# Root steps and sums of squares through PSUM, GpSimd's order pinned in one stage, the opening reordered, and a norm's two sums moved to VectorE

## The chip, the cores and the metric

One core of one Trainium2 chip. The metric is the time of one execution on the device, in microseconds (us), the median of three runs. Engines by the profile's names: PE is TensorE (its weight loads are PEld), DVE is VectorE, ACT is ScalarE, POOL is GpSimd, SP issues the DMAs. Matrix products accumulate in PSUM banks of 128 x 512 fp32; all else lives in SBUF.

## The reference

Two transformer blocks in fp32, on 512 positions of width 1024. The first has a sparse attention and a gated convolution that are merged, then a convolutional feed-forward net; the second has two mixer layers (grouped-query plus latent attention, then windowed attention). The change touches only norms, and the order of work around them:

```python
def rms_norm(x, g):
    xf = x.astype(jnp.float32)
    y = xf * lax.rsqrt(jnp.mean(xf * xf, axis=-1, keepdims=True) + NORM_EPS)
    return (y * g.astype(jnp.float32)).astype(x.dtype)
...
        h = rms_norm(x, norm1_g[l])
        proj = h @ w_in[l]
        ...
        g_a, g_b = jnp.split(jax.nn.sigmoid(g_merge), 2, axis=-1)
        x = x + (g_a * y_attn + g_b * y_conv) @ w_out[l]
        x = x + conv_ffn(rms_norm(x, norm2_g[l]), ffn_w_up[l], ffn_dw_w[l], ffn_dw_b[l], ffn_w_down[l])
    return rms_norm(x, final_g)
```

The first norm of the second block is taken of the first block's output, which is itself normed by `final_g`; so the kernel needs two sums per position there, of x*x and of x*x times the squared gain.

## The kernel before

The residual stream lies as eight tiles `X[k]` of 128 features by 512 positions. A matrix product is done by `mm3` (L121): each fp32 operand is split into a high and a low part, and three matmuls (L124 to L126) per 128 rows of weights sum up low times high, high times low and high times high. Weights come by `wload` (L97): a DMA brings a raw tile, ScalarE makes the high part (L110), and GpSimd or VectorE, by a rotating table `wpools`, subtracts it to get the low part (L111). A tile-scheduling framework orders the instructions of each engine by their readiness; inside `in_order(...)` the named engines keep the order in which the code is written, and `after_root()` holds what follows until the instruction in `root[0]`.

A norm goes in four steps. `Squares.add` (L220): ScalarE squares a tile (L222), and `put` lets VectorE add it to a running sum in SBUF (L212 for the first pair, L215 for the others); the last tile is kept apart. `sums` (L225): TensorE multiplies both parts with ones (L232), so that the sums over features stand one position per partition, 128 x 4 or 128 x 2 numbers. `rsqrt` and `newton` (L160 to L183): VectorE scales and adds eps (L183), takes a first guess by integer arithmetic (L164) and improves it in two rounds (L167 to L173), eight dependent small instructions, all in SBUF. `row_bcast` (L189): TensorE turns the roots into a row on all partitions, which `to_sbuf` copies (L195).

In the opening, TensorE multiplies four 128-column groups of weights: two in banks `pkv`, then `pkb[0]` and `pkb[1]`. The sums stand in the middle of `pkb[0]`'s matmuls, the broadcast behind them. The row R1 then scales `tkv` (L354) and `tkb` (L437), the latter of which frees the banks for the w_v product. `windows` (L153, L381) lays out the keys for the compression.

In the gates stage (`gates`, called with `in_order("PE", "DVE")`) 14 products `w_g` of 24 matmuls run, with two weight tiles each; between them VectorE and GpSimd add the taps of a 31-tap convolution. For the first channel tile ScalarE scales the shifted input (L487) and GpSimd adds it (L488); the order on GpSimd is the scheduler's.

In the first norm of the second block, `by_halves` runs the last product of the feed-forward net (w_dn) for the first 256 positions, eight blocks of rows of 12 matmuls with 256 columns, and then for the other 256. `down` adds each block to X (L842), squares it, and `Weighted` (L234) lets TensorE multiply the squares with a two-column weight (ones and squared gain) into bank `po` (L248). After a half come L850 to L852, the root, the broadcast, and `modulated` (L817 to L819) for eight tiles. While the root of a half is awaited TensorE goes on with the next half or with `key_values`. `attn_out` and `last_out`, further on, work by halves in the same way with `Squares`.

Of the kernel before, what the change touches and what calls it, by code (L numbers as in the profile page):

```python
# [43 lines left out]
def build(ctx, tc, I, out):  # L44
# [136 lines left out]
    def rsqrt(src, scale, eps):  # L181
        x = new("s", (128, 20))[:, :src.shape[1]]
        V.tensor_scalar(x, src, scale, eps, op0=OP.mult, op1=OP.add)  # L183
        return newton(x)
# [12 lines left out]

    class Squares:


        def __init__(self, a=0, b=512):
            self.c = slice(a, b)
            self.acc = self.last = None
# [16 lines left out]
        def add(self, src, scale=1.0):  # L220
            t = new("p")
            A.activation(t[:, self.c], src[:, self.c], AF.Square, scale=scale)  # L222
            self.put(t)

        def sums(self, bank="ps"):  # L225
            st = new(bank)
            n = (self.c.stop - self.c.start) // 128
            for x in (self.acc, self.last):
                for i in range(n):

                    a = self.c.start + 128 * i
                    PE.matmul(st[:, i:i + 1], x[:, a:a + 128], ones[:, 0:1], start=x is self.acc and i == 0,  # L232
                              stop=x is self.last, skip_group_check=True)
            return st[:, 0:n]  # L234

    class Weighted:


        def __init__(self, a, w):
            self.c, self.w, self.n, self.st = slice(a, a + 256), w, 0, new("po")  # L240

        def add(self, src):
            t = new("p")
            A.activation(t[:, self.c], src[:, self.c], AF.Square)
            k = self.n
            for i in range(2):

                PE.matmul(self.st[:, 2 * i:2 * i + 2], t[:, self.c][:, i * 128:(i + 1) * 128], self.w[:, k, :],  # L248
                          start=k == 0 and i == 0, stop=k == KT - 1, skip_group_check=True)
            self.n += 1  # L250
# [1122 lines left out]
```

## Time and profile before

| what | us |
|---|---|
| median of three runs | 1309.24 |
| lowest and highest of them | 1303.06, 1313.09 |
| the profiled execution | 1305.09 |
| its span, first to last instruction | 1303.1 |
| TensorE busy | 1248.2 |
| VectorE busy | 893.2 |
| GpSimd busy | 729.7 |
| ScalarE busy | 701.7 |

The mean granted clock of TensorE was 0.992 of full speed. The busy times are of the profiled execution. A row of a timeline gives the start and the length of an instruction in us, or of several alike in a row (x4), and in brackets how long its engine had been idle before it and whose instruction ended the wait. Since matmuls are pipelined, their rows overlap; the distance of their starts is what one costs.

### The profile page before, as it was taken

What the parts mean: (1) busy time and instruction counts of PE and PEld (TensorE: products, weight loads), DVE (VectorE), ACT (ScalarE), POOL (GpSimd) and SP (SyncE); (2) the same over time, 40 slices, a digit from 0 to 9 for tenths busy, and PEclk for the clock granted to TensorE, in tenths of its full rate; (3) what the DMA queues carried; (4) which work ended last, traced back from release to release, by engine and by line L of the source; (5) the groups of instructions that cost most, each with busy time, mean ns of one, the idle gap of its engine ahead of it and who ended that gap; (6) DMA issues with size and microseconds to landing.
All of it is one profiled execution on the core that took longest, in us unless ns stands there. A gap on an engine that the chain in (4) does not pass through costs nothing. (4 is left out here: it accounts for less than half of the span.)

```text
span 1303.1 us, 19296 instructions
## 1 busy us (share of the span) xinstructions
PE 1248.2 (96%) x6369; PEld 1039.2 (80%) x6369; DVE 893.2 (69%) x1967; ACT 701.7 (54%) x1487; POOL 729.7 (56%) x715
## 2 busy tenths in 40 slices
PE   7899999799999999999999999999999989999996
PEld 5878877688888888888888798877777788888886
DVE  7755767697645777776877358677787776655565
ACT  6756777334543444423443243586677646776654
POOL 4457785844644666565665513477565423676542
PEclk9999999899999999999999999999999999999998
DMA  6231011332443555587553501211111111111221
GB/s 209 78 97 58 33 59 33 122 98 87 124 123 97 161 170 161 163 252 240 165 162 87 160 16 40 72 39 50 47 60 42 41 50 57 57 57 57 67 72 65
DMA packets 71971, 124.74 MB, mean 96 GB/s; under 512 B 8256, under 2 KB 17344, under 8 KB 71872
## 3 DMA queue, kind: packets, MB, share of 16 engines
q1 hardware_dynamic: 71872, 123.52, 30.5%
q8 instruction: 50, 0.82, 0.3%
q14 instruction: 49, 0.40, 0.1%
HBM read 121.39 MB, written 2.10 MB: 95 GB/s over the span
## 5 line engine op out<-in xcount | busy, mean ns | idle before, releaser
L111 POOL TENSOR_TENSOR wl<-wr,wh 128x512 fp32r<-128x512 f32 (+2 forms) x215 | 281.9, 1314 | 266.7 <-ACT wh L110 208.9
L124 PE MATMUL pg<-h,wl 128*128 128x512 f32 x628 | 249.3, 397 | 2.8 <-POOL wl L111 2.7
L126 PE MATMUL pg<-h,wh 128*128 128x512 f32 x628 | 246.7, 393 | 0.0
L125 PE MATMUL pg<-h,wh 128*128 128x512 f32 x628 | 246.5, 393 | 0.0
L110 ACT ACTIVATE wh<-wr 128x512 fp32r<-128x512 f32 (+2 forms) x215 | 132.5, 618 | 174.9 <-PE pg L126 83.0
L124 PEld LDWEIGHTS pg<-h,wl 128*128 128x128 f32 x628 | 118.4, 188 | 26.6 <-POOL wl L111 4.1
L126 PEld LDWEIGHTS pg<-h,wh 128*128 128x128 f32 x628 | 118.4, 189 | 23.0
L125 PEld LDWEIGHTS pg<-h,wh 128*128 128x128 f32 x628 | 118.5, 189 | 22.2 <-issue 0.7
L111 POOL TENSOR_TENSOR m<-t,m 128x512 fp32r<-128x512 f32 (+1 forms) x67 | 89.5, 1336 | 80.4 <-ACT m L110 78.3
L304 DVE TENSOR_TENSOR t<-pt,t 128x512 fp32r<-128x512 f32 (+1 forms) x160 | 97.4, 631 | 27.0 <-ACT t L303 25.8
L309 PE MATMUL po<-t,h 128*128 128x512 f32 (+3 forms) x384 | 110.0, 364 | 4.3 <-DVE t L304 1.9
L124 PE MATMUL ps<-h,wl 128*128 128x512 f32 x260 | 103.4, 398 | 7.4 <-POOL wl L111 7.4
L126 PE MATMUL ps<-h,wh 128*128 128x512 f32 x260 | 102.0, 392 | 0.0
L125 PE MATMUL ps<-h,wh 128*128 128x512 f32 x260 | 102.0, 392 | 0.0
L303 ACT ACTIVATE t<-pt 128x512 fp32r<-128x512 f32 (+1 forms) x160 | 84.4, 552 | 22.8 <-PE pt L299 22.1
L309 PEld LDWEIGHTS po<-t,h 128*128 128x128 f32 x384 | 65.7, 188 | 28.8 <-ACT t L303 13.2
L299 PE MATMUL pt<-k,p 128*128 128x128 f32 x576 | 85.5, 273 | 2.7 <-POOL p L976 2.5
L299 PEld LDWEIGHTS pt<-k,p 128*128 128x128 f32 x576 | 69.0, 140 | 14.3 <-POOL p L976 5.0
L744 DVE CUSTOM_DVE_ANT_0 b<-b,z 128x512 f32<-128x512 f32 x48 | 75.4, 1572 | 0.0
L976 POOL TENSOR_SCALAR p<-p,s 128x512 f32<-128x512 f32 x64 | 45.5, 713 | 49.8 <-DVE s L975 49.7
L124 PEld LDWEIGHTS ps<-h,wl 128*128 128x128 f32 x260 | 49.2, 189 | 20.2 <-POOL wl L111 10.1
L110 ACT ACTIVATE m<-t 128x512 fp32r<-128x512 f32 (+2 forms) x78 | 46.9, 604 | 33.7 <-PE ps L124 12.9
(404 smaller groups left out, 3050.9 us busy)
## 6 DMA issues: line engine op xcount, KB each, us to landing
b<-ada_t SPq DMA_DIRECT2D x48, 256.0 KB, 3.2
z<-ada_t SPq DMA_DIRECT2D x48, 256.0 KB, 3.2
t<-w_up SPq DMA_DIRECT2D x44, 256.0 KB, 2.8
wr<-w_up SPq DMA_DIRECT2D x44, 256.0 KB, 2.7
wr<-w_g SPq DMA_DIRECT2D x32, 256.0 KB, 2.6
t<-w_dn SPq DMA_DIRECT2D x23, 256.0 KB, 2.7
wr<-w_br SPq DMA_DIRECT2D x16, 256.0 KB, 2.7
wr<-w_gt SPq DMA_DIRECT2D x16, 256.0 KB, 2.8
```

Of the source, the lines that this page charges most:

```text
L110: A.activation(hi[:, :z], raw[:, :z], AF.Copy)
L111: eng.tensor_sub(lo[:, :z], raw[:, :z], f(hi[:, :z]))
L124: PE.matmul(ps, ll, rh, start=start and i == 0, stop=False)
L125: PE.matmul(ps, lh, rl, start=False, stop=False)
L126: PE.matmul(ps, lh, rh, start=False, stop=stop and i == n - 1)
L299: PE.transpose(ps[:, o:o + 128], src, ident)
L303: evac[:] = [A.activation(hi[:, :n], ps[:, :n], AF.Copy)]
L304: evac.append(V.tensor_sub(lo[:, :n], ps[:, :n], f(hi[:, :n])))
L309: PE.matmul(o[:, a:b], v, t[:, pa:pa + b - a], start=start and z == 0, stop=stop and z == 1)
L744: V.tensor_tensor_reduce(out=raw, in0=raw, in1=CA[z], op0=OP.mult, op1=OP.add, scale=1.0, scalar=0.0, accum_out=MA[l][:, z, m:m + 1])
L976: scaled[0] = G.tensor_scalar(p, p, sm[:, 1:2], 0.0, op0=OP.mult, op1=OP.add)
```

## The change

Its parts, with the line numbers of the new kernel where they differ:

- `newton` (now L160 to L179) has eleven instructions: the guess is written twice (L168), to PSUM and to SBUF, the value after the first round too (L174), and one step is split in two (L177, L178). Its temporaries lie in columns of a PSUM bank, that of the sums or a new `po`.
- `Squares.add` writes the first square into a PSUM bank (`pt`), and VectorE adds the following ones there (L245); the add of the last but one goes to SBUF, and the last square goes to TensorE by itself as before. `sums` is L256 and its banks are `pt` or `po`.
- Opening: the sums come after two instead of four rows of `pkb[0]`, the w_v weights don't wait for the root, all eight of their low parts are GpSimd's, `tkb[0]` (L443) stands ahead of the windows.
- `gates(0, 7, ...)` is written under `in_order("Pool")` as well. Taps are L497 now.
- `down`: `Weighted` is gone; VectorE keeps a plain sum (L245) and a weighted sum (L856, L861) in two `pt` banks, and TensorE sums each once per half.

```diff
-    def newton(x):
+    def newton(x, bank=None):
         n = x.shape[1]
-        y = new("s", (128, 20))[:, :n]
-        t = new("s", (128, 20))[:, :n]
-        V.tensor_scalar(y.bitcast(I32), x.bitcast(I32), -0.5, float(0x5F3759DF), op0=OP.mult, op1=OP.add)
-        V.tensor_mul(t, y, y)
+        r, q, u = [new("s", (128, 20))[:, :n] for _ in range(3)]
+        st = bank or work[0]
+        y = st[:, 64:64 + n]
+        t = st[:, 128:128 + n]
+        for z in (y, r):
+            V.tensor_scalar(z.bitcast(I32), x.bitcast(I32), -0.5, float(0x5F3759DF), op0=OP.mult, op1=OP.add)
+        V.tensor_mul(t, y, r)
         V.scalar_tensor_tensor(t, t, -0.5 * 0.375, x, op0=OP.mult, op1=OP.mult)
-        V.scalar_tensor_tensor(y, t, 1.5 * 0.375, y, op0=OP.add, op1=OP.mult)
-        V.tensor_mul(t, y, y)
+        for z in (y, q):
+            V.scalar_tensor_tensor(z, t, 1.5 * 0.375, r, op0=OP.add, op1=OP.mult)
+        V.tensor_mul(t, y, q)
         V.scalar_tensor_tensor(t, t, 64.0 / 9, x, op0=OP.mult, op1=OP.mult)
-        V.scalar_tensor_tensor(t, t, -10.0 / 3, t, op0=OP.add, op1=OP.mult)
-        root[:] = [V.scalar_tensor_tensor(y, t, 5.0, y, op0=OP.add, op1=OP.mult)]
-        return y
+        V.tensor_scalar(u, t, -10.0 / 3, None, op0=OP.add)
+        V.tensor_mul(t, t, u)
+        root[:] = [V.scalar_tensor_tensor(r, t, 5.0, q, op0=OP.add, op1=OP.mult)]
+        return r
...
-        def add(self, src, scale=1.0):
+        def add(self, src, scale=1.0, bank="pt"):
+            i, c = self.n, self.c
+            self.n += 1
+            if i == 0:
+                self.sum = new(bank)
+                A.activation(self.sum[:, c], src[:, c], AF.Square, scale=scale)
+                return
             t = new("p")
-            A.activation(t[:, self.c], src[:, self.c], AF.Square, scale=scale)
-            self.put(t)
+            A.activation(t[:, c], src[:, c], AF.Square, scale=scale)
+            if i == self.of - 1:
+                self.last = t
+            else:
+                acc = self.sum
+                if i == self.of - 2:
+                    self.acc = new("z", (128, 542))[:, 0:512]
+                    acc = self.acc
+                V.tensor_add(acc[:, c], self.sum[:, c], t[:, c])
+            return t
...
-        mm3(pkb[0], wk[0][:4], xg[:4], True, False)
+        mm3(pkb[0], wk[0][:2], xg[:2], True, False)
         r1 = rsqrt(total.sums("pt"), 1.0 / D, EPS)
-        mm3(pkb[0], wk[0][4:], xg[4:], False, True)
+        mm3(pkb[0], wk[0][2:], xg[2:], False, True)
...
-    with after_root():
-        wv = wsplit(I["w_v"], KT, 280, ("m", "h"))
+    wpools[0] = [("t", "wh", "wl", G), ("wr", "wh", "wl", G)]
+    wv = wsplit(I["w_v"], KT, 280, ("m", "h"))
+    wpools[0] = [("t", "wh", "wl", G), ("t", "wh", "wl", V), ("wr", "wh", "wl", G)]
...
+    tkb = [new("p") for _ in range(2)]
+    root[:] = [V.tensor_mul(tkb[0], pkb[0], R1)]
     with after_root():
         ZK = windows(tkv[0], cv("pek", 0, 16))
-    tkb = []
-    for b in range(2):
-        tkb.append(new("p"))
-        V.tensor_mul(tkb[b], pkb[b], R1)
+    V.tensor_mul(tkb[1], pkb[1], R1)
...
     with in_order("PE", "DVE"):
-        gates(0, 7, 0, 90)
+        with in_order("Pool"):
+            gates(0, 7, 0, 90)
...
     def down(th, m, ps, c):
         if m == 0:
-            sums.append(Weighted(256 * th, fg2))
+            sums.append((Squares(256 * th, 256 * th + 256), new("pt")))
         V.tensor_add(X[m][:, c], X[m][:, c], ps)
-        sums[th].add(X[m])
+        total, weighted = sums[th]
+        t = total.add(X[m])
+        w = weighted[:, c]
+        if m == 0:
+            V.tensor_scalar(w, total.sum[:, c], fg2[:, m, 1:2], None, op0=OP.mult)
+            return
+        if m == KT - 1:
+            weighted = new("z", (128, 542))[:, 0:512]
+            sums[th] = (total, weighted)
+        V.scalar_tensor_tensor(weighted[:, c], t[:, c], fg2[:, m, 1:2], w, op0=OP.mult, op1=OP.add)
```

How the instructions stand now, at three places. First VectorE in the opening, before: from the copy of the row R1 (L195), which stands 15 instructions after the root's last, to the product that frees the first bank (L437).

```order
L195 COPY r_333<-pt_328 128x512
L372 TENSOR_TENSOR h_475<-k_107,h_474 128x8
L354 TENSOR_TENSOR p_360<-pg_208,r_333 128x512
L354 TENSOR_TENSOR p_362<-pg_209,r_333 128x512
L153 TENSOR_TENSOR p_421<-p_360,p_420 128x512
L381 CAST h_424<-p_420 64x8x31 x2
L381 CAST h_438<-p_420 64x8x31 x2
L437 TENSOR_TENSOR p_452<-ps_234,r_333 128x512
```

After: from the last three steps of the root to the same product (L443) and the first instruction of the windows.

```order
L177 TENSOR_SCALAR s_302<-pt_289 128x4
L178 TENSOR_TENSOR pt_289<-pt_289,s_302 128x4
L179 SCALAR_TENSOR_TENSOR s_300<-pt_289,s_301 128x4
L201 COPY r_337<-pt_332 128x512
L363 TENSOR_TENSOR p_364<-pg_208,r_337 128x512
L363 TENSOR_TENSOR p_366<-pg_209,r_337 128x512
L443 TENSOR_TENSOR p_424<-ps_234,r_337 128x512
L153 TENSOR_TENSOR p_428<-p_364,p_427 128x512
```

The three low parts (L111) and 11 small preparations that stood between root and copy are gone from there, and the product stands ahead of the windows.

Second, GpSimd at the start of the gates, before. The second gate product's low parts are `wl_2802` and `wl_2808`; they stand in the middle of the attention:

```order
L488 TENSOR_TENSOR h_1071<-h_1071,r_2088 128x512
L111 TENSOR_TENSOR wl_2760<-wr_2758,wh_2759 128x512
L111 TENSOR_TENSOR wl_2802<-wr_2800,wh_2801 128x512
L111 TENSOR_TENSOR wl_2808<-wr_2806,wh_2807 128x512
L475 TENSOR_SCALAR p_2167<-p_2167 128x512
```

and where the gates begin (`t_2797`, `t_2845` and so on are ScalarE's scaled taps):

```order
L488 TENSOR_TENSOR h_1071<-h_1071,r_2655 128x512
L488 TENSOR_TENSOR h_1071<-h_1071,t_2797 128x512
L488 TENSOR_TENSOR h_1071<-h_1071,t_2845 128x512
L111 TENSOR_TENSOR wl_2850<-wr_2848,wh_2849 128x512
L111 TENSOR_TENSOR wl_2856<-wr_2854,wh_2855 128x512
L488 TENSOR_TENSOR h_1071<-h_1071,t_2894 128x512
L111 TENSOR_TENSOR wl_2899<-wr_2897,wh_2898 128x512
L488 TENSOR_TENSOR h_1071<-h_1071,t_2942 128x512
L488 TENSOR_TENSOR h_1071<-h_1071,t_2991 128x512
L488 TENSOR_TENSOR h_1071<-h_1071,t_3039 128x512
L111 TENSOR_TENSOR wl_2905<-wr_2903,wh_2904 128x512
L488 TENSOR_TENSOR h_1071<-h_1071,t_3088 128x512
```

After, from the same place; the low parts of the second gate product are `wl_2806` and `wl_2812` here:

```order
L590 TENSOR_SCALAR p_2584<-p_2584,s_2616,k_519 128x512
L497 TENSOR_TENSOR h_1075<-h_1075,r_2659 128x512
L497 TENSOR_TENSOR h_1075<-h_1075,t_2801 128x512
L111 TENSOR_TENSOR wl_2806<-wr_2804,wh_2805 128x512
L111 TENSOR_TENSOR wl_2812<-wr_2810,wh_2811 128x512
L497 TENSOR_TENSOR h_1075<-h_1075,t_2849 128x512
L111 TENSOR_TENSOR wl_2854<-wr_2852,wh_2853 128x512
L111 TENSOR_TENSOR wl_2860<-wr_2858,wh_2859 128x512
L497 TENSOR_TENSOR h_1075<-h_1075,t_2898 128x512
L111 TENSOR_TENSOR wl_2903<-wr_2901,wh_2902 128x512
L111 TENSOR_TENSOR wl_2909<-wr_2907,wh_2908 128x512
L497 TENSOR_TENSOR h_1075<-h_1075,t_2946 128x512
```

One tap and two low parts alternate now, and the second product's low parts moved from the attention to a place behind the first tap.

Third, TensorE at the broadcast of the second half's root in the first norm of the second block (L189, L195 after). Before it stands in the second bank of `key_values`:

```order
L124 MATMUL pg_8061<-m_7756,h_7727 128x256
L125 MATMUL pg_8061<-m_7757,h_7726 128x256
L189 MATMUL pt_7975<-k_106,s_7965 128x128 x4
L126 MATMUL pg_8061<-m_7756,h_7726 128x256
L124 MATMUL pg_8061<-m_7762,h_7733 128x256
L125 MATMUL pg_8061<-m_7763,h_7732 128x256
L126 MATMUL pg_8061<-m_7762,h_7732 128x256
L124 MATMUL pg_8061<-m_7762,h_7739 128x256
```

After, it stands in the first bank of the queries (128x512), which follows it:

```order
L125 MATMUL pg_8096<-m_7786,h_7761 128x256
L126 MATMUL pg_8096<-m_7785,h_7761 128x256
L124 MATMUL ps_8133<-h_7791,h_7720 128x512
L125 MATMUL ps_8133<-h_7792,h_7719 128x512
L126 MATMUL ps_8133<-h_7791,h_7719 128x512
L124 MATMUL ps_8133<-h_7797,h_7726 128x512
L195 MATMUL pt_8010<-k_106,s_7996 128x128 x4
L125 MATMUL ps_8133<-h_7798,h_7725 128x512
```

The last seven matmuls of `key_values` and four of the queries moved ahead of the broadcast.

## Rows read from the trace of the kernel before

**Rows 1.** Busy table: engine, busy us, share of the span, instructions.
```profile
PE 1248.2 (96%) x6369; PEld 1039.2 (80%) x6369; DVE 893.2 (69%) x1967; ACT 701.7 (54%) x1487; POOL 729.7 (56%) x715
```

**Rows 2.** Waits of TensorE, whole span: us in total, times, longest us.
```profile
PE ps L124 <- POOL wl L111: 7.4, 6, 3.5
...
PE pt L189 <- DVE s L173: 5.4, 5, 2.1
PE ps L124 <- DVE p L437: 3.4, 1, 3.4
PE ps L232 <- DVE z L215: 3.4, 3, 2.1
PE pg L124 <- POOL wl L111: 2.7, 2, 2.2
...
PE po L189 <- DVE s L173: 1.0, 1, 1.0
```

**Rows 3.** Timeline of VectorE, opening: start, length, operation [idle before it].
```profile
25.46 0.16 DVE L183 TENSOR_SCALAR s<-pt 128x4 f32<-128x4 f32 x1 [0.77 <-PE pt L232]
...
28.15 0.70 DVE L171 SCALAR_TENSOR_TENSOR s<-s,s 128x4 f32<-128x4 f32 x1
...
30.24 3.40 DVE L111 TENSOR_TENSOR h<-t,m 128x280 fp32r<-128x280 f32 x3
...
39.55 0.69 DVE L437 TENSOR_TENSOR p<-ps,r 128x512 f32<-128x512 f32 x1
```

**Rows 4.** Timeline of TensorE, opening.
```profile
30.37 1.16 PE L189 MATMUL pt<-k,s 128*128 128x128 f32 x8 [2.08 <-DVE s L173]
...
36.60 0.39 PE L126 MATMUL ps<-h,wh 128*128 128x512 f32 x1
40.39 0.57 PE L124 MATMUL ps<-m,h 128*128 128x280 f32 x1 [3.40 <-DVE p L437]
```

**Rows 5.** Timeline of GpSimd, gates.
```profile
218.02 3.03 POOL L488 TENSOR_TENSOR h<-h,t 128x512 f32<-128x512 f32 x2 [10.61 <-ACT t L487]
...
231.27 5.37 POOL L488 TENSOR_TENSOR h<-h,t 128x512 f32<-128x512 f32 x4
...
246.99 3.73 POOL L111 TENSOR_TENSOR wl<-wr,wh 128x512 fp32r<-128x512 f32 x3
```

**Rows 6.** Timeline of ScalarE, gates.
```profile
217.17 1.32 ACT L487 ACTIVATE t<-z,k 128x512 f32<-128x512 f32 x2
```

**Rows 7.** Timeline of TensorE, gates.
```profile
217.02 0.39 PE L124 MATMUL pg<-h,wl 128*128 128x512 f32 x1
```

**Rows 8.** Windows, core 0: busy us of each engine (instructions), then granted clock.
```profile
225.50:231.00 5.50, 5.33 (x24) 4.09 (x22) 4.66 (x8) 4.59 (x8) 5.34 (x5) 1.00 0.18 60
238.00:241.00 3.00, 3.00 (x8) 2.33 (x9) 1.10 (x2) 1.68 (x4) 2.84 (x3) 0.51 0.32 87
768.50:787.40 18.90, 18.02 (x151) 17.73 (x151) 14.81 (x40) 11.06 (x26) 6.37 (x5) 1.00 0.16 39
```

**Rows 9.** The third step of the roots (L168): ns least/median/longest, first and last start.
```profile
L168 DVE SCALAR_TENSOR_TENSOR s<-s,s x12: 147/161/1249, 26.6 to 1294.3; 128x4 f32<-128x4 f32 x5, 128x2 f32<-128x2 f32 x4, 128x20 f32<-128x20 f32 x2, 128x8 f32<-128x8 f32 x1
```

**Rows 10.** Timeline of TensorE, first norm of the second block.
```profile
762.58 0.61 PE L248 MATMUL po<-k,p 128*128 128x2 f32 x4
763.05 0.36 PE L124 MATMUL pg<-h,h 128*128 128x256 f32 x1
...
764.62 0.49 PE L248 MATMUL po<-k,p 128*128 128x2 f32 x3
...
768.54 1.16 PE L189 MATMUL pt<-k,s 128*128 128x128 f32 x8 [1.06 <-DVE s L173]
...
787.40 0.38 PE L189 MATMUL pt<-k,s 128*128 128x128 f32 x1 [0.33 <-DVE s L173]
```

**Rows 11.** Timeline of VectorE, same stretch.
```profile
766.25 1.25 DVE L168 SCALAR_TENSOR_TENSOR s<-s,s 128x4 f32<-128x4 f32 x1
...
773.56 0.47 DVE L817 SCALAR_TENSOR_TENSOR p<-x,k,pt 128x256 f32<-128x256 f32 x1
```

More of the change, by code (lines that the diff above doesn't have):

```diff
@@ L179, in after_root, with rsqrt @@
         return tc.issue_after(getattr(root[0], "ins", root[0]))
-    def rsqrt(src, scale, eps):
+    def rsqrt(src, scale, eps, bank=None):
         x = new("s", (128, 20))[:, :src.shape[1]]
         V.tensor_scalar(x, src, scale, eps, op0=OP.mult, op1=OP.add)
-        return newton(x)
+        return newton(x, bank)
     def row_bcast(col, tag="ps"):
@@ L196, in to_sbuf, with __init__ @@
         return t
+    work = []
     class Squares:
-        def __init__(self, a=0, b=512):
-            self.c = slice(a, b)
+        def __init__(self, a=0, b=512, of=KT):
+            self.c, self.of, self.n = slice(a, b), of, 0
             self.acc = self.last = None
@@ L227, in sums @@
             n = (self.c.stop - self.c.start) // 128
-            for x in (self.acc, self.last):
+            parts = [x for x in (self.acc, self.last) if x is not None]
+            for x in parts:
                 for i in range(n):
                     a = self.c.start + 128 * i
-                    PE.matmul(st[:, i:i + 1], x[:, a:a + 128], ones[:, 0:1], start=x is self.acc and i == 0,
-                              stop=x is self.last, skip_group_check=True)
+                    PE.matmul(st[:, i:i + 1], x[:, a:a + 128], ones[:, 0:1], start=x is parts[0] and i == 0,
+                              stop=x is parts[-1], skip_group_check=True)
+            work[:] = [st]
             return st[:, 0:n]
[L236 to L250, printed above, removed]
     def stack_q(src, r0, scale):
@@ L353, in build @@
         t = new("p")
-        V.tensor_mul(t, pkv[b], R1)
+        root[:] = [V.tensor_mul(t, pkv[b], R1)]
         tkv.append(t)
@@ L691, in build @@
         PE.matmul(mp, ones, total.last, start=False, stop=True)
-        total = Squares()
+        total = Squares(of=4)
         for c in range(4):
@@ L721, in build @@
         total.add(X[m])
-    R2 = to_sbuf(row_bcast(rsqrt(total.sums(), 1.0 / D, EPS), "po"), "R'")
+    R2 = to_sbuf(row_bcast(rsqrt(total.sums("pt"), 1.0 / D, EPS), "po"), "R'")
     MD = [new("k", (128, 24), tag=f"md{l}") for l in range(2)]
@@ L834, in build @@
     fg2 = new("k", (128, KT, 2), tag="fg2")
-    V.memset(fg2[:, :, 0], 1.0)
     V.tensor_mul(fg2[:, :, 1], cv("fg", 0, 8), cv("fg", 0, 8))
@@ L848, in build @@
         t = new("s", (128, 16))[:, 0:2]
-        st = sums[th].st[:, 0:4].rearrange("p (i z) -> p z i", z=2)
-        V.tensor_scalar(v[:, 0:2], st[:, 0], 1.0 / D, EPS, op0=OP.mult, op1=OP.add)
+        total, weighted = sums[th]
+        V.tensor_scalar(v[:, 0:2], total.sums("po"), 1.0 / D, EPS, op0=OP.mult, op1=OP.add)
         V.tensor_scalar(t, v[:, 0:2], EPS, None, op0=OP.mult)
-        V.scalar_tensor_tensor(v[:, 2:4], st[:, 1], 1.0 / D, t, op0=OP.mult, op1=OP.add)
+        total.acc, total.last = weighted, None
+        V.scalar_tensor_tensor(v[:, 2:4], total.sums("pt"), 1.0 / D, t, op0=OP.mult, op1=OP.add)
         R = row_bcast(newton(v), "pt")
@@ L922, in build @@
         if i % 2:
-            rs = rsqrt(ss[:, 10 * i - 10:10 * i + 10], 1.0, EPS)
+            rs = rsqrt(ss[:, 10 * i - 10:10 * i + 10], 1.0, EPS, new("po"))
             for z in range(2):
@@ L941, in latent_inputs @@
             CN.append(cn)
-        rc = rsqrt(ss, 1.0, EPS)
+        rc = rsqrt(ss, 1.0, EPS, new("po"))
         for i, cn in enumerate(CN):
@@ L1126, in build @@
     for th, c in by_halves(I["w_eo"], 4, 8, OC[4:], attn_out, "m", ws):
-        R = row_bcast(rsqrt(sums[th].sums(), 1.0 / D, EPS), "pt")
+        R = row_bcast(rsqrt(sums[th].sums("po"), 1.0 / D, EPS), "pt")
         for k in range(KT):
@@ L1231, in build @@
     for th, c in by_halves(I["w_oo"], 4, 8, OC[4:], last_out, "m", ws):
-        R = row_bcast(rsqrt(sums[th].sums(), 1.0 / D, EPS), "pt")
+        R = row_bcast(rsqrt(sums[th].sums("po"), 1.0 / D, EPS), "pt")
         r0 = new("r", tag=("R", "R'")[th])[:, 0:256]
```

## The prediction

> **What bounds the kernel now.** I read the busy table first, then the waits of TensorE, then the timelines of the stretches in which those waits lie, then the order of instructions of both kernels. TensorE works for 1248.2 us of a span of 1303.1 us [rows 1]: only 55 us are idle, so a change that leaves the large matmuls as they are can win the idle places, and what a low clock adds behind them, and little else. [rows 2] says who ended the idle times: 7.4 + 2.7 us the low parts of weights that GpSimd subtracts (L111), 5.4 + 1.0 us the inverse roots (L173), 3.4 us one bank eviction (L437) and 3.4 us adds of squares (L215). The change touches each of them.
>
> **The reference time.** The sum is made against the profiled execution, 1305.09 us (the span and 2 us around it). The median of the three runs, 1309.24, is 4 us above it; they go from 1303.06 to 1313.09. I place the median after the change 1.5 us above what the sum gives.
>
> **The price of a root.** The kernel has twelve roots; an undisturbed step takes 161 ns (the median), the slowest 1249 [rows 9]. In the opening a 128x4 step takes 0.70 us [rows 3], in the first norm of the second block 1.25 us [rows 11], both while GpSimd subtracts weights. After the slow step, 766.25 to 767.50, five more end before the broadcast at 768.54 [rows 10]: 0.2 us from one dependent step to the next. The new root has 11 instructions for 8, and each step with two operands has one of them in PSUM. Undisturbed it costs more by something between 3 x 0.08 (the second writer of a value depends on nothing that the first does and overlaps it by half) and 3 x 0.2 us; I take 0.5. Where GpSimd is in the way it can win back the difference of 4.9 us (opening, 25.46 to 30.3, [rows 3, 4]) and 2.4. A step from PSUM to PSUM is not in the trace; the nearest row is the first step, which reads a PSUM bank: 0.16 us [rows 3], as from SBUF.
>
> [...]
>
> **Opening (gain 5.6).** The sums stand six 128x512 matmuls earlier. These start every 0.229 us (24 in 5.50 us, [rows 8]): 1.4 us. The root starts near 24.1 instead of 25.46 and, taking 2.4 us, ends near 26.5 instead of 30.3. TensorE ran dry at 30.37 - 2.08 = 28.3 [rows 4], so the wait of 2.08 goes (were the root as slow as before, 24.1 + 4.9 = 29.0, two thirds of it). Then TensorE fills the second bank until 36.99 and stands 3.40 us for L437 [rows 4], which VectorE reaches only at 39.55, behind three low parts (3.40 us, now GpSimd's), the row copy, two products and the windows [rows 3]. In the new order that product is the fourth operation after the root: broadcast 28.3 to 29.5 (1.16, [rows 4]), then copy and three products of 0.69 each, done near 32.2, while the second bank ends near 29.5 + 24 x 0.229 = 35.0. This wait goes too. [...] Together 2.1 + 3.4 + 1.2 = 6.7. The windows of the keys now start behind the product, which can cost their reader about 1 us. I take 5.6; bounds 1.4 and 6.7. GpSimd's three additional low parts, at most 1.1 us each by VectorE's time for them [rows 3], no longer wait for the root and are needed after 35.0 only; if they came late, the lower bound holds.
>
> **Gates, GpSimd's order (gain 4.0).** GpSimd adds conv taps (L488, 1.3 to 1.5 us) in runs of up to four, 5.37 us, ahead of the low parts that the next gemm needs [rows 5]. Four waits there make 6.8 us: the 2.7 of the pg banks, and 3.5 and 0.6 of the 7.4 of the ps banks, the rest of which lies in w_dn [rows 2]. Two are long enough to drop the clock: 2 x 1.2 more. So 9.2 us are to be had. Pinned, GpSimd has two low parts and one tap per gemm, 2 x 1.24 (3.73 for three) + 1.5 = 4.0 us [rows 5] against 24 x 0.229 = 5.5 of TensorE: later gemms don't wait. But the pin also puts the two low parts of the second gate gemm, which were done long before, behind a tap whose input ScalarE delivers at about 217.85 (two taps in 1.32 from 217.17, [rows 6]). The tap ends near 219.5, the first low part near 220.8; TensorE was ready at 217.02 [rows 7]: a new wait of 3.8 and 1.2 of clock behind it. 9.2 - 5.0 = 4.2; I take 4.0. Bounds 0 (each gemm loses a little) and 9.2 (ScalarE delivers sooner).
>
> **Second norm of the first block, R2 (gain 1.0).** The wait of 1.0 us for the root on the po bank [rows 2] is shorter than a stretched step, and its broadcast now stands five matmuls, 1.1 us, later. Bounds 0 and 1.0.
>
> **First norm of the second block (gain 2.0).** Removed: 16 groups of weighted sums on TensorE. Two groups start 2.04 us apart, and the next matmul starts 0.47 after a group [rows 10]: 16 x 0.47 = 7.5 us of TensorE. Added: on VectorE, per block of rows, an add and a multiply-add of 128x256, no longer than the 0.47 of the nearest row [rows 11]. In half 0 VectorE then has 3 x 0.47 = 1.4 us per block against 2.04 - 0.47 = 1.57 of TensorE, and keeps up: the eight blocks end 4 us earlier, the new sums follow them, and with an undisturbed root the broadcast comes near 765.6 instead of 768.54. In half 1 VectorE becomes the bound. Between the two broadcasts, 768.5 to 787.4, it was busy 14.81 of 18.90 us [rows 8]; fifteen new operations of 0.43 add 6.5: about 21, the second broadcast comes near 786.6, only 0.8 earlier, and TensorE, with about 13 us of work placed between them, stands idle some 7 us there. But that broadcast also stands later in TensorE's order, by 7 matmuls of 128x256 and 4 of 128x512, 1.75 us. 0.8 + 1.75, less 0.5 for the clock: 2.0. Bounds -3 (25 us between the broadcasts, and the clock) and +4.
>
> **Other places.** The halves of attn_out and last_out wait 3.4 us for adds of squares [rows 2] that have two SBUF operands while GpSimd subtracts; now one operand is in PSUM. I take 1.5; bounds 0 and 3.4. The last root has nothing to hide it: -0.5. The three roots of the head norms lie beside matmuls, which hide them: 0, and without that cover -1.5 or +1.5. The root of the conv norm ends no wait: 0.
>
> **Sum.** 5.6 + 4.0 + 1.0 + 2.0 + 1.5 - 0.5 = 13.6; 1305.1 - 13.6 = 1291.5; the median 1293.
>
> **The rivals.**
> First, the pin costs nothing at its start: ScalarE delivers the tap before 217 and all 9.2 us come back. For it, ScalarE idles at other times; against it, it delivers at 217.85 in the trace. 1293 - 5 = 1288.
> Second, VectorE takes it back: 25 us between the broadcasts (-3 for +2), windows that delay the opening (3 for 5.6), adds that win nothing (0 for 1.5): 1293 + 5 + 2.6 + 1.5 = 1302. For it, VectorE is already busy 14.81 of 18.90 us where it gets 6.5 more [rows 8]; against it, TensorE has other work in order there.
> [...]
> Fourth, slower: the strict order makes every gate gemm wait for ScalarE's tap as the second does. Twelve more gemms would stand; from 13.6 / 12 = 1.1 us each the change loses, and at 3.8 us the time is 1293 + 46 = 1339, at half of it 1316. For it, one late tap now holds two low parts. Against it, a tap takes ScalarE 0.66 us [rows 6] of the 5.5 us of a gemm.
>
> **How the numbers follow.** The forecast gets 0.50, the first rival 0.12, the second 0.23, the third 0.08, the fourth 0.07. A measurement of this kernel can tell about 1% from no change: under 1296.1 is faster by over 1%. Faster: 0.8 of the forecast (its own range is 1287 to 1299), all of the first rival, half of the third: 0.56. Slower by over 1%, above 1322: the greater part of the fourth, 0.05. Within 1%: the rest, 0.39. The range goes from 1281, the first rival with its bounds, to 1307, behind the second; the fourth is left outside.
>
> **What would show it.** Right: no wait at the first broadcast and none at the w_v gemm; one wait of 3 to 4 us at the second gate gemm and none at the twelve behind it; no step of a root near 1 us; some 7 us of idle TensorE in the second half of that first norm, ended by VectorE. Wrong: waits for L111 at each gate gemm, steps in PSUM of more than 0.25 us, or more than 23 us between the two broadcasts.

## The result: 0.6% faster, where about 1% was forecast

The changed kernel takes 1299.95 us (median of ten runs, 1297.53 to 1301.83) against 1306.8 for the kernel before (ten runs): a ratio of 0.9943, interval 0.9925 to 0.9961, so some 7 us less. The forecast was 1293 with a range of 1281 to 1307. The sign and the range hold, but the range reaches from 26 us faster to no change at all, so it tests little. The gain lies within 1%, to which the forecast gave 0.39. The sum had 13.6 us of gain; the kernel won about half of it.

The profiled execution took 1298.56 us, its span is 1296.7 us. TensorE's busy row [rows 1] and its waits [rows 2] after the change, the first from the busy table, the others from the view of waits (total us, times, longest):

```profile
PE 1242.9 (96%) x6329; PEld 1035.4 (80%) x6329; DVE 894.7 (69%) x2027; ACT 701.4 (54%) x1487; POOL 730.7 (56%) x718
```
```profile
PE pg L124 <- DVE m L111: 7.3, 1, 7.3
PE pg L124 <- DVE x L851: 5.7, 1, 5.7
PE pg L124 <- POOL wl L111: 3.9, 2, 3.7
PE po L256 <- DVE z L245: 3.1, 2, 2.9
PE ps L124 <- POOL wl L111: 2.9, 4, 1.4
...
PE pt L195 <- DVE s L179: 2.3, 1, 2.3
PE ps L124 <- DVE x L1141: 2.0, 1, 2.0
PE pg L124 <- ACT p L464: 2.0, 1, 2.0
```

Of the old waits those for L437 and R2 are gone, the roots' 5.4 are 2.3 (the last root alone), GpSimd's 7.4 + 2.7 are 6.8. In their place stand others: 5.7 us for an eviction of w_dn (L851), 3.7 us for one low part in the gates, 2.0 for an eviction of w_v (L464), 2.0 for one of attn_out (L1141; the kernel before waits 1.4 + 0.3 for the same operation, its L1122). The first two had been forecast, with their places; TensorE has 5 us less work and nearly the same idle time.

To see where time was won and lost, take an instruction that both kernels have and set its start in one trace against the other. Where the order of work has changed, the two must be taken at a place with the same work left. These are worked out from the two timelines (the last line from the spans); line numbers are those of the kernel before:

```
place                                         before   after   shift  this stage   forecast
behind the opening (TensorE, wait of 0.57)     63.97   60.76   -3.21     -3.2        -5.6
last gates (VectorE, eviction L646)           299.17  290.27   -8.90     -5.7        -4.0
behind the conv norm (TensorE, first L124)    318.75  310.52   -8.23     +0.7         0
w_dn, behind R2 (TensorE, wait for L111)      715.05  706.28   -8.77     -0.5        -1.0
behind the first norm (TensorE, L126)         840.72  831.86   -8.86     -0.1        -2.0
behind the head norms (TensorE, L126)         874.85  867.55   -7.30     +1.6         0
attention (TensorE, wait for L883)            907.92  900.59   -7.33      0.0         0
behind attn_out (VectorE, first L1168)       1099.46 1093.88   -5.58     +1.8   } -1.0 for
before the last norm (VectorE, L316)         1265.70 1260.20   -5.50     +0.1   } both norms
end                                           1303.1  1296.7   -6.40     -0.9
```

Opening and gates won 8.9 us together, less than forecast in one and more in the other. The first norm of the second block won next to nothing. The head norms and attn_out lost 3.4. These are single executions: the six profiled kernels with the same opening shift by 3.2 to 4.6 us there, and the one kernel whose opening is unchanged (e6) by 0.9 the other way, so a stage's figure is good to about 1 us.

**Opening.** VectorE's and ScalarE's timelines, then TensorE's, of the changed kernel [rows 3, 4]:

```profile
24.10 0.16 DVE L189 TENSOR_SCALAR s<-pt 128x4 f32<-128x4 f32 x1 [2.64 <-PE pt L256]
...
25.74 0.17 DVE L176 SCALAR_TENSOR_TENSOR pt<-pt,s 128x4 f32<-128x4 f32 x1
...
27.33 0.52 DVE L1218 TENSOR_SCALAR k<-k 128x16 f32<-128x16 f32 x1 [1.42 <-DMA k<-row]
...
28.15 0.16 DVE L179 SCALAR_TENSOR_TENSOR s<-pt,s 128x4 f32<-128x4 f32 x1
```
```profile
48.23 0.49 ACT L464 ACTIVATE p<-ps,s 128x280 f32<-128x280 f32 x1
48.62 0.49 ACT L464 ACTIVATE p<-pg,s 128x280 f32<-128x280 f32 x1
```
```profile
49.25 0.47 PE L124 MATMUL pg<-h,wl 128*128 128x512 f32 x1 [1.97 <-ACT p L464]
```

The root starts at 24.10, as forecast, and its steps are short, but a small operation of another part stands in its middle and waits 1.42 us for a DMA: it ends at 28.3, just in time, and neither of the old waits is there. Part of that is luck: the forecast had the end at 26.5, and in e4, with the same opening, TensorE waits 0.89 us for this root. What came instead is the wait at 49.25: ScalarE evicts the w_v products only at 48.2, behind the windows and the stacking of the keys. In the chain of the windows one product with two operands in SBUF (L153, at 32.09) takes 2.46 us beside GpSimd's subtractions, 0.69 before; what it adds to that wait was not tested.

**Gates.** GpSimd, then TensorE [rows 5, 7]:

```profile
214.81 1.67 POOL L497 TENSOR_TENSOR h<-h,t 128x512 f32<-128x512 f32 x1 [10.61 <-ACT t L496]
216.43 2.50 POOL L111 TENSOR_TENSOR wl<-wr,wh 128x512 fp32r<-128x512 f32 x2
218.89 1.27 POOL L497 TENSOR_TENSOR h<-h,t 128x512 f32<-128x512 f32 x1
```
```profile
217.75 0.79 PE L124 MATMUL pg<-h,wl 128*128 128x512 f32 x1 [3.74 <-POOL wl L111]
```

The tap waits for ScalarE, the low parts wait for the tap, TensorE 3.74 us for them: 3.8 had been forecast. No other gate product waits.

**First norm of the second block.** TensorE's broadcasts and its wait, VectorE at the eviction that it waits for, and the window between the broadcasts [rows 8, 10, 11]:

```profile
757.37 1.16 PE L195 MATMUL pt<-k,s 128*128 128x128 f32 x8
768.55 0.58 PE L124 MATMUL pg<-h,h 128*128 128x256 f32 x1 [5.72 <-DVE x L851]
...
780.42 1.05 PE L195 MATMUL pt<-k,s 128*128 128x128 f32 x8
```
```profile
766.35 1.43 DVE L111 TENSOR_TENSOR h<-wr,h 128x512 fp32r<-128x512 f32 x1
767.70 0.48 DVE L861 SCALAR_TENSOR_TENSOR pt<-p,k,pt 128x256 f32<-128x256 f32 x1
768.09 0.41 DVE L851 TENSOR_TENSOR x<-x,pg 128x256 f32<-128x256 f32 x1
```
```profile
757.40:780.40 23.00, 17.28 (x120) 16.92 (x121) 19.43 (x56) 10.85 (x25) 6.29 (x5) 0.85 0.13 35
```

The broadcasts stand 23.05 us apart instead of 18.86. The first came 11.2 us earlier than before, at the second it is 7.0. In between TensorE works 17.3 of 23 us at a granted clock of 0.85. The broadcasts shift by -7.0 here, but the products behind them stand at -8.9: the work that was placed ahead of the second broadcast is done by then.

**Head norms.** VectorE at the root of 128x8, first the kernel before, then the changed one:

```profile
837.58 0.16 DVE L164 TENSOR_SCALAR s<-s 128x8 int32<-128x8 int32 x1
...
840.00 0.17 DVE L173 SCALAR_TENSOR_TENSOR s<-s,s 128x8 f32<-128x8 f32 x1
```
```profile
828.71 0.16 DVE L168 TENSOR_SCALAR po<-s 128x8 int32<-128x8 int32 x1
...
832.13 0.17 DVE L177 TENSOR_SCALAR s<-po 128x8 f32<-128x8 f32 x1
832.21 1.44 DVE L276 CAST h<-h 64x512 fp32r<-64x512 f32 x1
833.68 0.17 DVE L178 TENSOR_TENSOR po<-po,s 128x8 f32<-128x8 f32 x1
833.89 0.68 DVE L266 SCALAR_TENSOR_TENSOR h<-pt,h 64x512 fp32r<-64x512 f32 x1
834.60 0.17 DVE L179 SCALAR_TENSOR_TENSOR s<-po,s 128x8 f32<-128x8 f32 x1
```

Each step is short, yet from first to last they take 5.9 us instead of 2.4: more steps leave more places where other operations of VectorE get in between. All nine profiled kernels with the new root here take 5.9 us, the three with the old one 2.4.

**attn_out.** ScalarE, TensorE and VectorE:

```profile
1043.17 0.63 ACT L110 ACTIVATE wh<-wr 128x512 fp32r<-128x512 f32 x1 [2.46 <-DMA wr<-w_ok]
1043.70 0.40 ACT L237 ACTIVATE p<-x 128x256 f32<-128x256 f32 x1
```
```profile
1044.70 0.58 PE L256 MATMUL po<-k,z 128*128 128x1 f32 x4 [2.86 <-DVE z L245]
```
```profile
1046.91 0.16 DVE L168 TENSOR_SCALAR po<-s 128x2 int32<-128x2 int32 x1
1046.99 0.67 DVE L168 TENSOR_SCALAR s<-s 128x2 int32<-128x2 int32 x1
```

The adds are short now, yet the sum waits 2.86 us instead of 2.09: the square in front of it stands in ScalarE's queue behind a weight whose transfer has not landed. And the root has become longer; the evictions of attn_out (L1141) stand behind its end at 1049.37, and TensorE waits for them and for the operation that follows (L829) 2.0 + 0.8 us, against 1.4 + 0.3.

### The profile page after: what moved, and what is told of

It is laid out like the page before. It is cut to its first block, busy times and chain, and to the rows that moved or that the text cites. A ratio compares the mean times of both kernels' runs of the same rounds, so it can differ in the third digit from the quotient of the medians.

```text
span 1296.7 us, 19271 instructions
## 1 busy us (share of the span) xinstructions
PE 1242.9 (96%) x6329; PEld 1035.4 (80%) x6329; DVE 894.7 (69%) x2027; ACT 701.4 (54%) x1487; POOL 730.7 (56%) x718
## 5 line engine op out<-in xcount | busy, mean ns | idle before, releaser
L111 POOL TENSOR_TENSOR wl<-wr,wh 128x512 fp32r<-128x512 f32 (+2 forms) x215 | 281.7, 1314 | 256.6 <-ACT wh L110 199.3
L111 POOL TENSOR_TENSOR m<-t,m 128x512 fp32r<-128x512 f32 (+1 forms) x67 | 89.2, 1331 | 72.9 <-ACT m L110 69.8
L318 PEld LDWEIGHTS po<-t,h 128*128 128x128 f32 x384 | 65.7, 188 | 29.2 <-ACT t L312 13.6
L124 PE MATMUL pg<-h,m 128*128 128x512 f32 (+1 forms) x144 | 56.4, 391 | 7.3 <-DVE m L111 7.3
```

The source lines that it names most:

```text
L111: eng.tensor_sub(lo[:, :z], raw[:, :z], f(hi[:, :z]))
L124: PE.matmul(ps, ll, rh, start=start and i == 0, stop=False)
L318: PE.matmul(o[:, a:b], v, t[:, pa:pa + b - a], start=start and z == 0, stop=stop and z == 1)
```

## The experiments

Ten kernels were run, several times each, beside the kernel before. All are edits of the changed kernel but one. Ratios are to the kernel before; the changed kernel's is 0.9943. The median of the kernel before went from 1304.98 to 1306.8 us between these comparisons, so a difference of two medians below is uncertain by 1 to 2 us. The shifts quoted are made as in the table above, on TensorE at the same work left.

**e1, the first norm as before.** The class `Weighted` and the old `down` are back:

```diff
-            sums.append((Squares(256 * th, 256 * th + 256), new("pt")))
+            sums.append(Weighted(256 * th, fg2))
...
-        V.tensor_scalar(v[:, 0:2], total.sums("po"), 1.0 / D, EPS, op0=OP.mult, op1=OP.add)
+        V.tensor_scalar(v[:, 0:2], st[:, 0], 1.0 / D, EPS, op0=OP.mult, op1=OP.add)
```

> The changed kernel with the first norm of the second block as before (weighted sums on TensorE, 64 small matmuls), all else as changed. My theory: in the second half VectorE's 15 added operations delay the evictions and the root, TensorE stands 5.7 us for an eviction, and the stage loses about 2 us against the kernel before; then this kernel is 1.5 to 3 us faster than the changed one, about 1298, and the broadcast of the second half stands some 2 us earlier against the rest. Rival: the loss there comes from the longer root or the low clock, not from the sums on VectorE; then the time stays within 0.5 us of the changed kernel or grows by what half 0 had won (up to 4 us).

Measured: 1298.58 us (1295.29 to 1305.4), 0.9951 [0.9934, 0.9969]. The median is 1.4 us below the changed kernel's, less than the runs spread, and the two ratios lie inside each other's interval. The wait for L851 is gone, but in the profiled execution, which took 1304.03, the shift goes from -6.0 to -4.1 across the stage, 1.9 us lost without any wait of over 0.3 us: the clock was low there (window 740 to 790, same columns as above). Behind it the head norms lose 1.6 as in the changed kernel.

```profile
740.00:790.00 50.00, 49.74 (x348) 47.77 (x347) 24.87 (x76) 18.14 (x42) 8.01 (x6) 0.90 0.09 24
```

So this run decides nothing by itself; e2 does for the second half, and e3 for the rival's longer root.

**e2, half 0 on VectorE, half 1 on TensorE.**

```diff
     def down(th, m, ps, c):
+        if th:
+            if m == 0:
+                sums.append(Weighted(256, fg2))
+            V.tensor_add(X[m][:, c], X[m][:, c], ps)
+            sums[1].add(X[m])
+            return
         if m == 0:
```

> The changed kernel, with the weighted sums of the first half on VectorE as changed and those of the second half on TensorE as before. My theory: the gain is in half 0 (some 3 to 4 us less TensorE work beside an idle VectorE) and the loss in half 1, so this one is the best of the three: 3 to 5 us faster than the changed kernel, 1295 to 1297, with no wait of over 2 us for an eviction in half 1. Rival: half 0 wins nothing, because the root of half 0 is bound by the same chain; then it is like the kernel with both on TensorE, within 1 us.

Measured: 1294.12 us (1293.57 to 1294.2), 0.9908 [0.9891, 0.9925]: 5.8 us below the changed kernel, no wait for an eviction or a root in the stage. The window over both halves, 745 to 780:

```profile
745.00:780.00 35.00, 34.98 (x275) 33.80 (x275) 26.34 (x80) 16.49 (x38) 8.24 (x6) 1.00 0.13 35
```

TensorE is busy all the time at full clock, and the shift goes from -8.3 to -14.5 across the stage: 6.2 won, where the changed kernel wins 0.1. So the gain is in half 0, and half 1 gives it back. Behind it e2 loses 1.6 at the head norms and 3.3 at attn_out.

**e3, the old root.**

```diff
-        r, q, u = [new("s", (128, 20))[:, :n] for _ in range(3)]
-        st = bank or work[0]
...
+        y = new("s", (128, 20))[:, :n]
+        t = new("s", (128, 20))[:, :n]
```

> The changed kernel with the root of before: eight steps, all operands in SBUF. My theory: undisturbed the new root takes 2.4 us instead of 1.7, and where TensorE waits for a root (halves of the three norms, six times) that is paid, so this kernel is 2 to 4 us faster, 1296 to 1298, unless GpSimd stretches a step there. Rival: the PSUM operands are what keeps the steps short; then steps of 0.7 to 1.2 us come back in at least three of the twelve roots and the time is 1 to 4 us longer, 1301 to 1304.

Measured: 1298.69 us (1296.04 to 1301.39), 0.9946 [0.9925, 0.9966]: not to be told from the changed kernel. Both theories are right, in different places, and they cancel. The stretched steps are back, here in the first norm:

```profile
758.03 0.16 DVE L172 SCALAR_TENSOR_TENSOR s<-s,s 128x4 f32<-128x4 f32 x1
758.23 1.18 DVE L173 SCALAR_TENSOR_TENSOR s<-s 128x4 f32<-128x4 f32 x1
759.44 0.16 DVE L174 SCALAR_TENSOR_TENSOR s<-s,s 128x4 f32<-128x4 f32 x1
```

with waits of TensorE for the root of 0.79 (opening), 0.96 (R2) and 1.20 (first norm) that the changed kernel has not. But the wait for the last root is 1.8 instead of 2.3, the head norms lose nothing (-7.3 on both sides), and attn_out keeps its shift (-7.0 to -7.1) where the changed kernel goes from -7.3 to -5.6. So the new root is what the head norms and attn_out lose by: 1.6 and 1.7 us. At the first norm the old root wins 0.4 (-6.9 to -7.3), so the root's length isn't what half 1 loses by.

**e4, the taps one product later.**

```diff
-            for t in rest[len(rest) * i // len(todo):len(rest) * (i + 1) // len(todo)]:
+            for t in rest[len(rest) * max(i - 1, 0) // len(todo):len(rest) * i // len(todo)]:
                 conv_tap(0, t)
+        for t in rest[len(rest) * (len(todo) - 1) // len(todo):]:
+            conv_tap(0, t)
```

> The changed kernel with each conv tap of GpSimd written one gate product later, so that the two low parts of the second gate product no longer stand behind the first tap. My theory: the wait of 3.7 us at the second gate product and the low clock of 1.2 us behind it go, and no other comes: 4 to 5 us faster, 1295 to 1296. Rival: GpSimd has no slack there and the wait moves to the third or fourth product: 0 to 1 us.

Measured: 1294.61 us (1292.06 to 1296.36), 0.9911 [0.9889, 0.9933]. No gate product waits, and the shift goes from -4.7 to -15.9 across the gates: 11.2 us won instead of 5.7, so the order of the second product is worth 5.5 us there, about what was expected.

**e5, the old opening**, with the new root and squares: four rows before the sums, `tkb` behind the windows, the w_v weights behind the root.

> The changed kernel with the opening as before (sums after four rows, w_v weights behind the root, the product that frees the first bank behind the windows), but with the new root and squares. My theory: the opening is worth 3.2 us of the 6.7 it removes, because the windows' work on ScalarE and VectorE then ends last and TensorE waits 2 us for ScalarE's eviction of w_v; so this kernel is 2.5 to 4 us slower than the changed one, 1302 to 1304, and has waits of 3 to 4 us before the w_v product and none of 2 us for that eviction. Rival: the shorter root alone would have closed the first wait; then it is 0 to 1.5 us slower.

Measured: 1300.45 us (1297.86 to 1302.82), 0.9957 [0.9943, 0.9971]. Only 0.5 us above the changed kernel, 1.8 by the ratios; in the profile the shift behind the opening is -0.9 instead of -3.2 (-3.5 to -4.6 in the other profiles with the new opening). The wait at the first broadcast is gone without the earlier sums, so the new root closed that one by itself; the wait for the bank remains:

```profile
38.23 0.57 PE L124 MATMUL ps<-m,h 128*128 128x280 f32 x1 [2.92 <-DVE p L446]
```

The times of whole runs don't settle whether the opening's edits are worth 0.5 or 2 us; the profiles speak for 2.3 to 3.7.

**e6, the pin alone** in the kernel before:

```diff
-        gates(0, 7, 0, 90)
+        with in_order("Pool"):
+            gates(0, 7, 0, 90)
```

> The kernel before with GpSimd's order pinned in the gates and nothing else. My theory: the gates were worth 5.7 us in the changed kernel, and its 3.7 us wait comes from the second product's low parts standing behind a tap; in this kernel these two stand ahead of the tap of that product, so the wait may be smaller: 5.5 to 10 us faster than before, 1296 to 1300. Rival: without the other parts the scheduler places taps so that GpSimd stays late: under 4 us.

Measured: 1301.26 us (1298.82 to 1307.85), 0.9979 [0.996, 0.9999]. In the profile (1299.78) the gates shift by 5.6 us and the wait of 3.74 at the second product is there as well, so the pin makes both, whatever else is changed. The median gains less than that (4.3 us against the kernel before), as three of the ten runs took 1306 or more, at a mean clock of 0.984 instead of 0.991.

**e7, other buffers for w_ok.**

```diff
-    wpools[0] = [("wr", "wh", "wl", G)]
+    wpools[0] = [("t", "wh", "wl", G)]
     KO = []
```

> The changed kernel with the raw tiles of w_ok in another pool of buffers than the weights before them, so that their transfers need not wait until VectorE and GpSimd have split those. My theory: in the first half of attn_out ScalarE stands 2.5 us for such a transfer ahead of a square, and TensorE 2.9 us for the sum; with the transfer early both go and the stage gains 1.5 to 3 us: 1297 to 1298.5. Rival: the squares are bound by VectorE's blocks there; then under 0.5 us.

Measured: 1299.52 us (1297.81 to 1302.32), 0.9961 [0.9948, 0.9974], no gain. The wait for the sum is gone, and others are in its place; the stage still loses 2.2 us (-4.3 to -2.1):

```profile
1041.65 0.39 PE L124 MATMUL pg<-h,h 128*128 128x256 f32 x1 [0.70 <-POOL h L111]
...
1045.12 0.39 PE L124 MATMUL ps<-h,h 128*128 128x256 f32 x1 [1.77 <-DVE h L111]
```

The rival was right: the transfer only came last, and the splits of weights on VectorE and GpSimd stand right behind it. What the stage loses against the kernel before is not this wait but the longer root, as e3 shows.

**e8, three parts together**: e2, e4, and the old root in attn_out and last_out only.

> The changed kernel with three parts of the earlier runs: weighted sums of the second half on TensorE, taps of GpSimd one product later, and the old root in attn_out and last_out only, where nothing stretches it. If the places are independent: 1300 - 5.8 - 5.3 - 2 = about 1287 (1285 to 1290), 1.3 to 1.6% faster than before. Rival: what is won in one place is lost to transfers further on, as the shifts of the earlier runs shrink at attn_out: 1290 to 1293.

Measured: 1286.38 us (1284.96 to 1287.43), 0.9853 [0.9825, 0.988]. By the ratios that is 11.8 us below the changed kernel, where e2 has 4.6 and e4 4.2; the third part, the old root, was not run there by itself. With the old root there attn_out loses 1.1 us, where e2 and e4 lose 3.3 and 4.4.

**e9, sums of squares in SBUF again**, on e1:

```diff
-            A.activation(t[:, c], src[:, c], AF.Square, scale=scale)
...
+            A.activation(t[:, self.c], src[:, self.c], AF.Square, scale=scale)
+            self.put(t)
```

> The kernel of e1 (first norm as before), and the running sums of squares of all norms in SBUF as before as well; the roots, the pin and the opening as changed. My theory: sums in PSUM are worth little, since where an add was stretched by GpSimd (attn_out, last_out, opening) another wait stands right behind it (blocks late by GpSimd's and VectorE's splits, ScalarE's square behind a transfer): within 1 us of e1, with adds of 0.7 to 1.6 us back in the timeline and waits for z of up to 2 to 3 us in attn_out in both. Rival: the adds in PSUM carry the gain of attn_out and last_out; then 2 to 4 us slower than e1.

Measured: 1299.08 us (1296.46 to 1303.68), 0.9944 [0.9921, 0.9967]; e1 was 1298.58, so no difference that can be measured in whole runs. The long adds are back in the timeline, and the sum of attn_out waits 3.8 us instead of 2.9, that of last_out 1.2:

```profile
1038.82 1.39 DVE L223 TENSOR_TENSOR z<-z,p 128x256 f32<-128x256 f32 x1
1042.24 1.65 DVE L223 TENSOR_TENSOR z<-z,p 128x256 f32<-128x256 f32 x2
...
1270.15 1.72 DVE L223 TENSOR_TENSOR z<-z,p 128x256 f32<-128x256 f32 x2
```

Against e1 that costs 0.7 us at attn_out and some 1.6 at last_out. But the sums in PSUM cost as much elsewhere: at the conv norm e9 loses nothing, e1 2.3 us, and R2 goes from -8.5 to -9.8 where e1's shift gets 0.3 worse. All nine profiled kernels with the sums in PSUM have this wait of 0.50 at the conv norm, here the changed kernel's:

```profile
309.60 1.05 PE L256 MATMUL ps<-k,p 128*128 128x1 f32 x8 [0.50 <-ACT p L237]
```

So by these profiles the sums in PSUM are not without effect: what they win in the second block they lose in the first.

**e10, e8 with the w_v products evicted first**: the loop that stacks the keys (`KB`) is written behind the four w_v products.

> The kernel of e8, with the stacking of the keys (ScalarE and VectorE, 64x512) written behind the four w_v products, so that ScalarE evicts these products first. My theory: the 2 us wait of TensorE in the opening, which took back a third of what the opening had won, is ScalarE's queue; it goes, with the low clock behind it: 2 to 3.5 us faster than e8, 1283 to 1284.5. Rival: the keys are needed next, and the wait moves behind the convolution's first products: under 0.7 us.

Measured: 1285.53 us (1282.01 to 1287.66), 0.9835 [0.9798, 0.9872]. The wait of 1.97 for L464 is gone, but the next one (at the compression's product) is 1.12 instead of 0.57, and the shift behind the opening is -4.5 against -3.6. These 0.9 us are within what openings of the same order differ by, so nothing is shown to be won. This is the fastest kernel of the study, not to be told from e8.

## Why the prediction was right in sign and too large in size

**Opening: 3.2 instead of 5.6.** Both old waits went, the first only just. The 1.2 in its sum of 6.7 is for the low clock, and the kernel before has it there: behind the wait for L437, from 40.4 to 44 us, the granted clock is 0.57 and matmuls of 128x280 start 0.23 us apart, at full clock 0.13; that is about 1.3 us. The failed step is "the windows of the keys now start behind the product, which can cost their reader about 1 us": it cost 2.0 and a low clock behind it (0.66 from 50 to 55 us). Where 5.5 us of waiting leave TensorE's chain, the next chain is only so far behind, here ScalarE's evictions. e10 takes this wait away, and the one 10 us later, which was 0.57 in both kernels, grows to 1.12. And e5 shows that the first of the two waits did not need the earlier sums, only the undisturbed root; the prediction had said "two thirds of it" for the opposite case, the sums alone.

**Gates: 5.7 instead of 4.0.** The wait of 3.8 at the second product was forecast to 0.1 us and its cause is shown by e4. Mis-sized was the low clock, "2 x 1.2": the 1.2 is what eight matmuls lose in the row from 238 to 241 us [rows 8], 3.00 us instead of 8 x 0.229, but in the kernel before the granted clock is 0.51 from 238 to 241.5 us and 0.50 from 248.3 to 251.6 (0.83 over 235 to 255), about 1.7 us lost behind each wait. The new wait has 1.7 of it behind it as well. That makes 6.8 + 3.4 - 3.7 - 1.7 = 4.8; of the 5.7 measured, 0.9 was not traced.

```profile
238.00:242.00 4.00, 4.00 (x11) 3.16 (x12) 1.10 (x2) 2.62 (x5) 3.84 (x4) 0.57 0.24 66
248.00:252.00 4.00, 3.70 (x9) 2.98 (x10) 3.48 (x6) 1.10 (x2) 3.11 (x4) 0.57 0.66 216
```

**R2: 0.5 won instead of 1.0, and 0.7 lost at the conv norm.** The wait of 1.0 went, but two of 0.45 and 0.50 for ScalarE's last square came, one here and one at the conv norm. The prediction had set the conv norm at 0: it looked for waits that end, and the sums' new place in the order made one. Its price goes with the clock: in three of the nine profiles with this wait the granted clock is 1.00 over the 5 us behind it and the stage loses 0.7, in six it is 0.66 to 0.69 and the stage loses 2.2 to 2.3.

**First norm: 0.1 won instead of 2.0.** The mechanism stands as forecast: half 0 wins, VectorE bounds half 1, TensorE idles 5.7 us for the eviction. The first broadcast comes 2.4 us earlier against the rest (2.9 forecast), and "1.75" for the second one's later place came too: its shift is -7.0, that of the products behind it -8.9. The failed step is the distance of the broadcasts, "about 21", which is 23.05, just over the 23 that the prediction had named as a sign of being wrong. Fifteen operations of 0.43 were counted, but VectorE's own three splits of weights in this stretch took 1.43, 0.68 and 1.00 us, and it is busy 19.4 us only: 3.6 are waits inside the dependent chain. e2 shows the remedy, the sum on the engine that has time in each half. This was the second rival, in a weaker form and in this place alone.

**Head norms: 1.6 lost, where nothing was forecast.** "The three roots of the head norms lie beside matmuls, which hide them: 0" is the step that failed; the sentence's own alternative, "without that cover -1.5", is what came. The eleven steps were priced as if they stood alone; among other operations they took 5.9 us instead of 2.4. With the old root (e3) the loss is gone.

**attn_out and last_out: 0.9 lost instead of 1.0 won.** "I take 1.5" for the adds was half right: last_out won 1.6 before its root (the first step of the last root starts at 1286.65, before at 1293.74, a shift of 7.1 against 5.5 ahead of it), and the last root cost 0.5, as forecast. attn_out lost 1.8. Its adds are as short as hoped, which is worth 0.7 us (e9), but the sum waits for a transfer and, when that is moved (e7), for the splits. What loses is the root. The sum priced the last root alone, though attn_out's two stand on the chain as well and were put at nothing without a reason: in half 0 the root goes from 1046.72 to 1049.37, 2.65 us against 1.66 before, and 0.67 of that is the one step that still has all its operands in SBUF. With the old root the loss is gone (e3).

**The root.** Undisturbed it takes 2.2 us for 1.7, +0.5 as forecast. In the last root the second writing of the guess starts 0.07 us behind the first, that of the first round's value 0.20. The steps in PSUM never exceed 0.19 us:

```profile
L172 DVE SCALAR_TENSOR_TENSOR po<-po,s x7: 168/168/187, 797.4 to 1287.3; 128x2 f32<-128x2 f32 x4, 128x20 f32<-128x20 f32 x2, 128x8 f32<-128x8 f32 x1
```

against 1249 ns for the slowest of before [rows 9]. The third rival, with 0.08 of the chances, was that an operand in PSUM makes each step longer by enough to show in the time. No run shows that: the medians are 168 ns here and 161 with all operands in SBUF, and in the last root the dependent steps start 0.20 us apart in both kernels. So the third rival falls. One step was left exposed, the second writing of the first guess, which reads and writes SBUF, so the forecast "no step of a root near 1 us" did not hold:

```profile
L168 DVE TENSOR_SCALAR s<-s x12: 156/160/979, 24.4 to 1286.9; 128x4 int32<-128x4 int32 x5, 128x2 int32<-128x2 int32 x4, 128x20 int32<-128x20 int32 x2, 128x8 int32<-128x8 int32 x1
L168 DVE TENSOR_SCALAR po<-s x7: 156/164/175, 796.0 to 1286.8; 128x2 int32<-128x2 int32 x4, 128x20 int32<-128x20 int32 x2, 128x8 int32<-128x8 int32 x1
```

The same operation with the same input takes up to 979 ns into SBUF and never above 175 into PSUM. In the changed kernel's trace only SBUF-to-SBUF steps of a root stretch: besides this one the scaling ahead of it (L189), which takes up to 1070 ns from SBUF and at most 164 from PSUM.

The sum came out about 7 us too large: the opening, the first norm and R2 won some 5 us less than forecast, the head norms, the conv norm and the halves of attn_out and last_out came out 4 worse, and the gates, 1.7 better than forecast, covered part of it. That the sign held rests mostly on the gates. The first rival, no cost of the pin, did not come, nor did the fourth, every gate product waiting: one waits. What stays open: how much of the opening's edits shows in whole runs (0.5 to 2 us, where the profiles show more), 0.9 us of the gates, and what would win in attn_out beyond the old root, where e7 only moved the wait.

## What to carry to other kernels

When a wait is taken from the critical engine, look for the second-latest releaser at that place and at the next place where the engines meet; the gain ends there (in the opening 5.5 us of waits went and one of 1.97 came). Work moved from a full engine to one that is "69% busy" must fit in the stretch where it lands, half by half. A longer chain of dependent steps costs more than its own steps, as other work gets in between (in the head norms 5.9 us instead of 2.4); price it at each place where it stands. Where an instruction order is pinned, write what the next product needs ahead of what waits for another engine: that was worth about 5 us here, against some 7 for the whole change.

## What the runs showed of the hardware that was not expected

The spread of the runs goes with TensorE's clock. The changed kernel's ten runs go from 1297.53 us at a mean granted clock of 0.992 to 1301.83 at 0.988, e1's from 1295.29 at 0.994 to 1305.4 at 0.986. And the clock fell without a wait of over 0.3 us: in e1's profile TensorE is busy 49.74 of 50 us between 740 and 790, and the granted clock is 0.90 over it, about half from 775 to 780, in the half where small weighted matmuls stand between matmuls of 256 columns. e9's profile, with the same first norm, shows the same: 49.74 of 50 us busy between 735 and 785, clock 0.90, and 0.50 from 770 to 775. A similar order of work ran at full clock in e2 and in the kernel before; what makes the difference was not found.

Even a short wait can stand before a low clock, but not in every execution: the wait of 0.50 at the conv norm is the same in nine profiles, and the granted clock over the 5 us behind it is 0.66 to 0.69 in six and 1.00 in three. In the changed kernel, then in e1:

```profile
310.00:315.00 5.00, 5.00 (x30) 4.36 (x31) 3.13 (x14) 1.37 (x2) 1.06 (x2) 1.00 0.19 57
```
```profile
310.00:315.00 5.00, 5.00 (x20) 4.12 (x21) 1.90 (x12) 0.00 (x0) 0.62 (x1) 0.66 0.17 55
```
